# Router on raw rows, expert ranks on 32 partitions, layer 2's expert input by one-hot products

## The chip, the cores and the metric

The kernel runs on one core of one Trainium2 chip. The metric is the device time of one execution in microseconds (us). Three runs of the kernel before are given; where one trace is read, it is one further execution of the same kernel, recorded by the hardware profiler.

## The reference, cut to what matters

Two layers (`DEPTH` 2) over 256 latent tokens (`x`) and 256 context tokens (`ctx`) of width 1024. The context is only needed in the first layer, so layer 0 works on 512 tokens (4 tiles of 128) and layer 1 on 256 (2 tiles). In each layer a mixer gives `y`, and then:

```python
h = layer_norm(alpha * h + g1 * y, ln_g[i, 0], ln_b[i, 0])
f = hier_moe(h * (1 + sc2) + sh2, ...)          # the part that the change is about
h = layer_norm(alpha * h + g2 * f, ln_g[i, 1], ln_b[i, 1])
...
def hier_moe(h, ...):                            # 4 groups of 8 experts, 1024 -> 256 -> 1024
    lg = h @ w_grp + b_grp;  g_sel = argmax(lg)  # one group for each token
    le = h @ w_exp + b_exp                       # 32 expert scores
    top_v, top_i = top_k(le within g_sel, 2)     # two experts for each token
    combine = softmax(top_v) * p_grp
    y += combine[e] * (silu(h @ w_gate[e]) * (h @ w_up[e])) @ w_down[e]
```

With `xhat = (row - mean) * rstd`, the input of the router and of the experts is `xhat * gcol + bcol`, a scale and a shift for each of the 1024 columns that hold `ln_g`, `ln_b`, `sc2` and `sh2`.

## The kernel before

The text counts layers as the code does: `l = 0` and `l = 1` (the change's "layer 2" is `l = 1`). A scheduler places every instruction when the kernel is built; each engine then works through its own list in order, so that an instruction that waits holds back all that stand behind it on its engine.

**Out-projection.** The mixer's output goes through `w_out` in products of 128x512, split into a high and a low part (`ohi`, `olo`), so that three products make one block (lines 191, 192, 193). The halves n = 0 and n = 1 of a tile's 1024 columns are separate sums. After each half, `done(T, n, ps)` (in `post_mixer`) multiplies by the gate `g1` (L1948) and adds to the residual rows `xh` (L1950, L1952) on DVE.

**Normalization and router.** After the half n = 1 of tile T, `ln_stats` gives mean and rstd (`mv`), `ln_scaled` makes the scaled rows `h2` in two operations on 128x1024 (L976, L979), `moe_token_tile` stores `h2` to memory (`h2D`), turns it by 8 transposes (L1026) and multiplies by the router's weights `wr` in 8 fp32 products with 36 columns (L1030; each shows as two records). `ln_hat` writes `xhat` over `xh` on ACT (L984), and `moe_residual` (L1346) multiplies by `alpha * ln_g` and adds `alpha * ln_b` on POOL.

**Routing.** `moe_route` is a chain of small DVE operations: top group, top two experts, one-hot tables `OH`, the counts of each expert (products with the triangle `tri` and with ones), the rank of each expert by count (a compare of all 32 with all 32 on every partition, `big`, L1117 and L1118), the slot of each token's two choices (`slot`, L1139), and tables `idx`, `wt`, `tok`, made by products with one-hot `hl` (L1160, L1161). `perm` is the order of the experts by count.

**Experts.** `plan(l)` packs the experts by rank in passes of one, two or four experts, each pass with 128 slots. Layer 1 has 11 passes. Six experts' weights lie on chip when the routing ends (`SIX`); the others are loaded by SP (three loads of 1 MB each: gate, up, down) as the slots of earlier passes come free. The input of a pass is gathered by row from `h2D` (POOL, indirect DMA) and turned by 8 transposes (L1286). In layer 1 the first three passes (`CHIP1`) instead get theirs by `moe_near`: products of `h2` with a one-hot table `sel` in fp32, 32 records of 128x384 (L1277), after the slots are known. Within a pass, the products of `up` (L1295) run interleaved with the rest of the pass before: turn (L1311), `down` (L1321), sums (L1334); `between` sets that order, and the input of the next pass stands between `down` and the sums.

Of the kernel before, what the change touches and what calls it, by code (L numbers as in the profile page):

```python
# [8 lines left out]
F32 = mybir.dt.float32  # L9
# [9 lines left out]
D = 1024  # L19
# [6 lines left out]
SIX = 6  # L26
# [69 lines left out]
def consts():  # L96
# [55 lines left out]
class Trunk:  # L152
# [784 lines left out]
    def ln_cols(self, l, pool):  # L937
# [4 lines left out]
        o = pool.tile([128, 2, 2, 8], F32, name="lno", tag="lno")  # L942
        eng = nc.gpsimd if l else nc.scalar
        pk = lambda z: z.rearrange("(p k) -> p k", k=8)

        for r in range(2):
            eng.dma_start(c[:, r, 0], pk(self.modD[l][2, r, 0:1024]))
            eng.dma_start(c[:, r, 1], pk(self.modD[l][1, r, 1024:2048]))
        eng.dma_start(g[:, 0], pk(A['ln_g'][l, 0]))
        eng.dma_start(g[:, 1], pk(A['ln_b'][l, 0]))  # L950
        self.gD = gD = self.dp.tile([2, 2, 1024], F32, name=f"gD{l}")
        for r in range(2):
            V.tensor_scalar(c[:, r, 0], c[:, r, 0], 1.0, None, op0=OP.add)
            V.tensor_tensor(o[:, r, 0], g[:, 0], c[:, r, 0], op=OP.mult)
            V.tensor_tensor(o[:, r, 1], g[:, 1], c[:, r, 0], op=OP.mult)
            V.tensor_tensor(o[:, r, 1], o[:, r, 1], c[:, r, 1], op=OP.add)
            for q in range(2):
                eng.dma_start(pk(gD[r, q]), o[:, r, q])
# [28 lines left out]
    def moe_open(self, l, nT):  # L987
# [3 lines left out]
        nc.scalar.dma_start(self.wr[:], A['moe_wr'][l].rearrange("(k p) n -> p k n", p=128))  # L991
        self.br = self.lp.tile([128, 36], F32, name="br")
        self.bcast_row(self.br[:], A['moe_br'][l])
        self.mc = mw.tile([128, 108 + 128 * max(nT, SIX // 2)], F32, name="mc")
# [3 lines left out]
        nc.scalar.dma_start(self.tri[:], A['tri'])  # L998
        self.lg = mw.tile([128, nT, 36], F32, name="lg")
        self.wt = mw.tile([128, 16], F32, name="wt")  # L1000
# [13 lines left out]
        self.h2D = self.dp.tile([128 * nT, D], F32, name=f"h2D{l}")  # L1014
# [3 lines left out]
    def moe_token_tile(self, T, h2, hT):  # L1018

        nc = self.nc  # L1020
        nc.scalar.dma_start(self.h2D[128 * T:128 * T + 128, :], h2)
        for q in range(2):
            pt = self.ps(tag="tr", bufs=2)
            for k in range(4):
                c = 512 * q + 128 * k
                nc.tensor.transpose(pt[:, 128 * k:128 * k + 128], h2[:, c:c + 128], self.ident[:])  # L1026
            self.evac(hT[:, 4 * q:4 * q + 4].rearrange("p a b -> p (a b)"), pt[:], 'a')
        pl = self.ps(tag=("rd", "po")[T % 2], bufs=1)
        for k in range(8):
            nc.tensor.matmul(pl[:, 0:36], hT[:, k], self.wr[:, k], start=k == 0, stop=k == 7)  # L1030
        return lambda: nc.vector.tensor_tensor(self.lg[:, T], pl[:, 0:36], self.br[:], op=OP.add)

    def moe_route(self, l, nT):
# [55 lines left out]
        OH = self.OH  # L1089
        pb = rp.tile([128, 2, nn], F32, name="pb")  # L1090
# [3 lines left out]
        cum = rp.tile([128, nT + 1, 32], F32, name="cum")  # L1094
        both = t(32)
        V.memset(cum[:, 0], 0.0)
        V.tensor_tensor(both[:].rearrange("p t e -> p (t e)"), OH[:, 0], OH[:, 1], op=OP.add)
        for T in range(nT):
            V.tensor_tensor(cum[:, T + 1], cum[:, T], both[:, T], op=OP.add)
        ones = rp.tile([128, 128], F32, name="ones")  # L1100
        V.memset(ones[:], 1.0)
        pn = self.ps()
        nc.tensor.matmul(pn[:, 0:32], ones[:], cum[:, nT], start=True, stop=True)
        pc = self.ps()
        nc.tensor.matmul(pc[:, 0:nn], self.tri[:], both[:].rearrange("p t e -> p (t e)"), start=True, stop=False)
        nc.tensor.matmul(pc[:, 0:nn], ones[:], cum[:, 0:nT].rearrange("p t e -> p (t e)"), start=False, stop=True)

        n1, n2, n4 = WIDE[l]
        cnt, cap = self.cnt, self.cap
        key, rk, b0, t0, t1 = [rp.tile([128, 32], F32, name=n) for n in ("key", "rk", "b0", "t0", "t1")]  # L1110
        big = rp.tile([128, 32, 32], F32, name="big", tag="scr")
        row = lambda z: z.unsqueeze(1).to_broadcast([128, 32, 32])
        col = lambda z: z.unsqueeze(2).to_broadcast([128, 32, 32])
        V.tensor_copy(cnt[:], pn[:, 0:32])
        V.tensor_tensor(key[:], cnt[:], self.mc[:, 32:64], op=OP.mult)
        V.tensor_tensor(key[:], key[:], self.mc[:, 64:96], op=OP.add)
# [3 lines left out]
        V.tensor_scalar(t0[:], rk[:], float(-SIX), 0.0, op0=OP.add, op1=OP.max)  # L1120
        V.tensor_scalar(t0[:], t0[:], float(n1), 64.0, op0=OP.min, op1=OP.mult)
        V.scalar_tensor_tensor(b0[:], rk[:], 64.0, t0[:], op0=OP.mult, op1=OP.add)
        V.tensor_scalar(t0[:], rk[:], float(-SIX - n1 - n2), 0.0, op0=OP.add, op1=OP.max)
# [941 lines left out]
```

## Time and profile before

| | us |
|---|---|
| three runs | 1253.11, 1259.41, 1261.16 (median 1259.41) |
| the profiled execution | 1256.68, its span 1255.0 |
| PE busy | 1022.0 (81%) |
| DVE busy | 600.7 (48%) |
| ACT, POOL busy | 314.4 (25%), 317.3 (25%) |
| DMA queue q1 (weights, SP) | 291.05 MB |
| DMA over the span | 315.66 MB, mean 252 GB/s |

The profiled execution took 1.7 us more than its span. The shares of busy time are averages over stages with different limits: out-projection and expert stage of each layer keep PE or the DMA engines full, and between them lie the heads of the expert stages (normalization, router, routing), in which neither is.

### The profile page before, as it was taken

To read this page: it belongs to the slowest core of one execution; us is meant where nothing else is said; L and a number is where in the kernel's file an instruction comes from. 1 tells how busy PE (TensorE), PEld (TensorE's weight loads), DVE (VectorE), ACT (ScalarE), POOL (GpSimd) and SP (SyncE) were. 2 spreads that over 40 slices of the span, in tenths; PEclk is the share of its full clock that TensorE was granted. 3 is DMA by queue.
4 is the path that set the end of the run, shared out by engine and by line. 5 is a ranking of instruction groups with operands and counts; after the bars stand their busy time and mean duration, and the time that the engine had idled before them with its cause. 6 is when DMAs were issued, how large, how long until landed. Compare 5 with 4: busy or idle time off the path is not lost. (4 is left out here: it accounts for less than half of the span.)

```text
span 1255.0 us, 15029 instructions
## 1 busy us (share of the span) xinstructions
PE 1022.0 (81%) x5440; PEld 568.0 (45%) x5440; DVE 600.7 (48%) x1193; ACT 314.4 (25%) x614; POOL 317.3 (25%) x308
## 2 busy tenths in 40 slices
PE   5679757799899728787777889998999739989775
PEld 2468544355576623232232336655666625433221
DVE  5274894475654861111011172265768574443325
ACT  3143210322443311110000127242346221111001
POOL 7715674263001521110110064014201130000000
PEclk9879978699999959988888889999999859999888
DMA  8442615668295546989999863486344854999992
GB/s 306 168 120 60 216 39 164 181 241 272 70 339 189 221 174 263 410 345 387 408 394 401 326 228 97 159 326 210 120 198 172 318 201 187 411 386 418 419 421 94
DMA packets 78574, 315.66 MB, mean 252 GB/s; under 512 B 15119, under 2 KB 21407, under 8 KB 50272
## 3 DMA queue, kind: packets, MB, share of 16 engines
q1 hardware_dynamic: 61312, 291.05, 60.7%
q0 software_dynamic: 8096, 14.68, 4.2%
q10 hardware_dynamic: 9088, 8.94, 2.3%
q8 instruction: 44, 0.72, 0.2%
q14 instruction: 34, 0.28, 0.1%
HBM read 309.01 MB, written 16.37 MB: 259 GB/s over the span
## 5 line engine op out<-in xcount | busy, mean ns | idle before, releaser
L1295 PE MATMUL ps_mm<-wgu,xT 128*32 128x512 f32 (+2 forms) x960 | 230.8, 651 | 36.9 <-DMA wgu<-in_moe_w_up_dram 36.3
L1295 PEld LDWEIGHTS ps_mm<-wgu,xT 128*32 128x32 f32 (+2 forms) x960 | 58.1, 134 | 151.7 <-issue 140.5
L186 DVE TENSOR_TENSOR wlo<-raw,whi 128x1024 fp32r<-128x1024 f32 (+1 forms) x40 | 50.7, 1275 | 50.7 <-ACT whi L181 50.4
L181 ACT ACTIVATE whi<-raw 128x1024 fp32r<-128x1024 f32 (+1 forms) x42 | 41.5, 999 | 120.4 <-PE ps_rd L192 38.0
L1263 POOL DMA_INDIRECT xg<-h2D,idx x23 | 27.1, 1176 | 151.8 <-PE ps_mod L1334 102.2
L1429 POOL DMA_INDIRECT YD<-ys,dst x13 | 13.1, 1009 | 203.7 <-DVE ys L175 177.7
L193 PE MATMUL ps_mm<-ah,wlo 128*128 128x512 f32 x128 | 51.1, 408 | 14.9 <-DVE wlo L186 14.9
L1321 PE MATMUL ps_mod<-wdn,aT 128*32 128x512 f32 (+2 forms) x240 | 58.1, 674 | 1.0 <-DVE aT L175 1.0
L191 PE MATMUL ps_mm<-ah,whi 128*128 128x512 f32 x128 | 54.7, 430 | 0.8 <-ACT whi L181 0.8
L192 PE MATMUL ps_mm<-al,whi 128*128 128x512 f32 x128 | 52.4, 410 | 0.0
L1321 PE MATMUL ps_rd<-wdn,aT 128*32 128x512 f32 (+2 forms) x240 | 49.2, 593 | 0.0
L192 PE MATMUL ps_mm<-wlo,ah 128*128 128x512 f32 x92 | 39.1, 425 | 9.6 <-DVE wlo L186 8.1
L175 DVE COPY aT<-ps_po 128x256 f32<-128x256 f32 x26 | 11.0, 425 | 71.7 <-PE ps_po L1311 71.7
L1311 PE MATMUL ps_po<-ident,act 128*128 128x128 f32 x52 | 14.3, 363 | 35.6 <-DVE act L1303 35.4
L175 DVE COPY ys<-ps_rd 128x512 f32<-128x512 f32 x13 | 9.0, 692 | 66.7 <-PE ps_rd L1321 66.7
L174 ACT ACTIVATE ys<-ps_mod 128x512 f32<-128x512 f32 x13 | 7.8, 597 | 131.7 <-PE ps_mod L1321 131.7
L1452 DVE COPY dst<-idx 128x1 int32<-128x1 int32 x13 | 1.9, 153 | 80.8 <-DMA YD<-ys,dst 80.8
L193 PE MATMUL ps_mm<-whi,al 128*128 128x512 f32 x92 | 38.6, 419 | 0.6 <-POOL al L669 0.6
L191 PE MATMUL ps_mm<-whi,ah 128*128 128x512 f32 x92 | 38.7, 424 | 0.0
L1346 POOL TENSOR_TENSOR xh<-xh,wdn 128x1024 f32<-128x1024 f32 x12 | 31.3, 2619 | 28.3 <-ACT xh L984 23.6
L181 ACT ACTIVATE ysr<-t 128x512 fp32r<-128x512 f32 x20 | 12.6, 631 | 102.8 <-DVE t L1423 102.8
L175 DVE COPY xT<-ps_tr 128x512 f32<-128x512 f32 (+1 forms) x27 | 18.1, 672 | 38.4 <-PE ps_tr L1286 31.6
(632 smaller groups left out, 2301.8 us busy)
## 6 DMA issues: line engine op xcount, KB each, us to landing
wgu<-in_moe_w_gate_dram SPq DMA_DIRECT2D x60, 1024.0 KB, 7.7
wgu<-in_moe_w_up_dram SPq DMA_DIRECT2D x60, 1024.0 KB, 7.8
wdn<-in_moe_w_down_dram SPq DMA_DIRECT2D x60, 1024.0 KB, 7.6
raw<-in_mod_w_dram SPq DMA_DIRECT2D x24, 1024.0 KB, 5.4
raw<-in_w_in_dram SPq DMA_DIRECT2D x20, 1024.0 KB, 5.2
cc<-in_mod_w_dram SPq DMA_DIRECT2D x16, 1024.0 KB, 5.1
raw<-in_mod_w_dram SPq DMA_DIRECT2D x12, 512.0 KB, 4.8
wgu<-in_w_out_dram SPq DMA_DIRECT2D x4, 1024.0 KB
```

What stands on the lines that cost most here:

```text
L175: return nc.vector.tensor_copy(out, in_)
L181: nc.scalar.activation(hi, x, AF.Copy)
L186: return (nc.gpsimd if leng == 'p' else nc.vector).tensor_tensor(lo, x, hi.bitcast(F32), op=OP.subtract)
L191: mm(ps, l[0], r[0], start=start, stop=False)
L192: mm(ps, l[0], r[1], start=False, stop=False)
L193: mm(ps, l[1], r[0], start=False, stop=stop)
L1263: return self.nc.gpsimd.indirect_dma_start(out=xg, out_offset=None, in_=self.h2D[:], in_offset=bass.IndirectOffsetOnAxis(ap=gi, axis=0), b ...
L1295: self.nc.tensor.matmul(ps[s, :], xT[:, k, s], wts[j][0][:, :, k, :], start=k == 0, stop=k == 7, tile_position=(0, w * j))
L1311: nc.tensor.transpose(pt[:, 128 * k:128 * k + 128], act[:, k::2], self.ident[:])
L1321: self.nc.tensor.matmul(py[s, :], aT[:, k, s], wts[j][1][:, k, 512 * n:512 * n + 512], start=k == 0, stop=k == 1, tile_position=(0, w * j))
L1346: self.nc.gpsimd.tensor_tensor(self.xh[:, T], self.xh[:, T], rows[i], op=op)
L1429: nc.gpsimd.indirect_dma_start(out=self.YD[:], out_offset=bass.IndirectOffsetOnAxis(ap=dst, axis=0), in_=y[:], in_offset=None, bounds_chec ...
```

## The change

- **Router on un-normalized rows.** `router` makes `wrg = wr * gcol` (DVE) and, by products, the constants `lgc` (`gcol` and `bcol` times `wr`): 16 products of 36 columns for each stream, two streams in layer 0, one in layer 1. `router_half` runs after each half of a tile on the raw rows: 4 transposes, a copy, 4 products of 36 columns. The logits are then corrected with mean and rstd by two small operations on DVE. `wr` is laid out so that 576 bytes in a row go to a partition in each piece, where it was 144.
- **`ln_scaled` and the store to `h2D`** remain in layer 0 alone. In layer 1, `hi` and `lo` are the two parts of `xhat` in fp32r (ACT and DVE).
- **Ranks with the experts on partitions.** Counts as a row and as a column (products with ones), a 32x32 compare, and products that spread slot base, end and capacity to all partitions. The operations on 128x1024 are gone.
- **Residual.** Tiles 0 and 1 of layer 0 stay on POOL; tiles 2 and 3 of layer 0 and both tiles of layer 1 are called after the routing and run on DVE, as do three memsets of `xg` in layer 0. Layer 1's memsets are gone.
- **Layer 1's expert input.** All 11 passes by `moe_near`, now 4 products in fp32r for each of 8 column groups, with `gcol` and `bcol` applied in two copies out of PSUM. The first three passes are picked right after the counts (`near`, `sel`), before ranks and slots; the other eight by `moe_pick` from `slot`. The gathers and their transposes are gone there.

```diff
+    def router(self, l, streams):
...
+        for r in streams:
+            w = self.wrg[r] = self.lp.tile([128, 8, 36], F32, name=f"wrg{r}")
+            V.tensor_tensor(w[:], self.wr[:], self.gcol[:, r, 0].unsqueeze(2).to_broadcast([128, 8, 36]), op=OP.mult)
+            c = self.lgc[r] = self.lp.tile([128, 2, 36], F32, name=f"lgc{r}")
+            ps = self.ps(tag="po", bufs=1)
+            for q in range(2):
+                for k in range(8):
+                    nc.tensor.matmul(ps[:, 36 * q:36 * q + 36], self.gcol[:, r, q, k:k + 1].to_broadcast([128, 128]),
+                                     self.wr[:, k], start=k == 0, stop=k == 7)
+            V.tensor_copy(c[:, 0], ps[:, 0:36])
+            V.tensor_tensor(c[:, 1], ps[:, 36:72], self.br[:], op=OP.add)
...
+    def router_half(self, T, r, n, x, hT):
...
+        for j in range(4):
+            nc.tensor.transpose(pt[:, 128 * j:128 * j + 128], x[:, 512 * n + j:512 * n + 512:4], self.ident[:])
+        self.evac(hT[:].rearrange("p a b -> p (a b)"), pt[:], 'a')
+        pl = self.ps(tag=("rd", "po")[n], bufs=1)
+        for j in range(4):
+            nc.tensor.matmul(pl[:, 0:36], hT[:, j], self.wrg[r][:, 4 * n + j], start=j == 0, stop=j == 3)
...
+        pc = self.ps()[:, 0:nn]
+        mm(pc, self.tri[:], both[:].rearrange("p t e -> p (t e)"), start=True, stop=False)
...
+        if l:
...
+            V.scalar_tensor_tensor(near[:], both[:, :, 0:SIX], -1000.0, p3[:, :, 0:SIX], op0=OP.mult, op1=OP.add)
...
+            self.moe_near(sel, self.xT)
...
+        V.tensor_scalar(gt[:], kr[:], kc[:], None, op0=OP.is_lt)
+        pr_ = self.ps()
+        mm(pr_[0:32, 0:32], self.ones[0:32, 0:32], gt[:], start=True, stop=True)
+        mm(pr_[0:32, 32:33], gt[:], self.ones[0:32, 0:1], start=True, stop=True)
...
-        V.tensor_tensor(big[:], row(key[:]), col(key[:]), op=OP.is_gt)
-        V.tensor_reduce(rk[:], big[:], axis=AX.X, op=OP.add)
...
+    def moe_near(self, sel, xT):
...
         for k in range(8):
             pt = self.ps(tag="tr", bufs=2)
             for T in range(2):
-                nc.tensor.matmul(pt[:, 0:n], self.h2[T][:, k::8], sel[:, T], start=T == 0, stop=T == 1)
-            self.evac(self.xT[:, :, k], pt[:, 0:n].rearrange("p (i s) -> p i s", i=CHIP1))
+                for i, z in enumerate((self.hi[T][:], self.lo[T][:])):
+                    self.nc.tensor.matmul(pt[:, 0:n], z[:, k::8], sel[:, T], start=T == 0 and i == 0, stop=T == 1 and i == 1)
...
         if l:
+            self.moe_residual(range(nT), self.lrow, nc.vector)
             self.early((4, 1), (5, 0), (5, 1))
         else:
+            self.moe_residual((2, 3), self.lrow, nc.vector)
+            self.early((1, 1))
...
-            x = (lambda: self.moe_xT(src, xT(i + 1))) if near <= i + 1 < N else None
...
+            elif l and CHIP1 <= i + 1 < N:
+                sel = self.moe_pick(passes[i + 1][1], xp)
+                x = lambda: self.moe_near(sel, xTs(i + 1))
```

What the diff does not tell is where the scheduler puts the moved instructions. DVE in layer 0, around the start of the routing (L979 is the second operation of `ln_scaled`, L1031 the logits), before:

```order
L979 SCALAR_TENSOR_TENSOR wdn<-wdn,mv,B 128x1024
L1031 TENSOR_TENSOR lg<-ps_rd,br 128x36
L983 SCALAR_TENSOR_TENSOR mv<-mv 128x1
L1031 TENSOR_TENSOR lg<-ps_po,br 128x36
L1051 TENSOR_REDUCE rt_3441<-lg 128x4
L1096 MEMSET cum 128x32
```

The same place after (L987 is that second operation, L2017 and L2018 the corrected logits, L1389 the residual, L1083 the first operation of the routing):

```order
L987 SCALAR_TENSOR_TENSOR wdn<-wdn,mv,B 128x1024
L2018 SCALAR_TENSOR_TENSOR lg<-lg,mv,lgc_3001 128x36
L2023 SCALAR_TENSOR_TENSOR mv<-mv 128x1
L1389 TENSOR_TENSOR xh<-xh,wdn 128x1024
L1411 MEMSET xg_3495 128x1024
L1411 MEMSET xg_3496 128x1024
L1411 MEMSET xg_3497 128x1024
L1083 TENSOR_REDUCE rt_3505<-lg 128x4
L1389 TENSOR_TENSOR xh<-xh,wdn 128x1024
L1084 TENSOR_TENSOR rt_3506<-lg,rt_3505 128x16
```

One more L1389 stands before L987 and one more behind L1084: the four residual operations and the three memsets stand in front of the routing's first steps and between them, although the code calls them after it.

DVE in layer 1, the same place, before:

```order
L979 SCALAR_TENSOR_TENSOR xh<-xh,mv,B 128x1024
L1031 TENSOR_TENSOR lg<-ps_rd,br 128x36
L983 SCALAR_TENSOR_TENSOR mv<-mv 128x1
L1031 TENSOR_TENSOR lg<-ps_po,br 128x36
L1051 TENSOR_REDUCE rt_7182<-lg 128x2
```

After:

```order
L2018 SCALAR_TENSOR_TENSOR lg<-lg,mv,lgc_7017 128x36
L2023 SCALAR_TENSOR_TENSOR mv<-mv 128x1
L1389 TENSOR_TENSOR xh<-xh,wdn 128x1024
L2028 TENSOR_TENSOR lo_6996<-xh,hi_6994 128x1024
L1083 TENSOR_REDUCE rt_7289<-lg 128x2
L1389 TENSOR_TENSOR xh<-xh,wdn 128x1024
L1084 TENSOR_TENSOR rt_7290<-lg,rt_7289 128x8
L1093 TENSOR_TENSOR rt_7296<-lg,rt_7289 128x8
L1389 TENSOR_TENSOR xh<-xh,wdn 128x1024
L1085 TENSOR_TENSOR rt_7290<-rt_7290,mc 128x8
L1389 TENSOR_TENSOR xh<-xh,wdn 128x1024
```

The four residual operations of layer 1 and the low part `lo` of tile 1 now stand among the first steps of the routing; the first residual operation needs the row `ln_g` (tile `wdn`) loaded by SP and scaled by ACT.

PE in layer 1's expert stage, one pass, from `down` to the sums, before (`xg` is a gathered tile):

```order
L1321 MATMUL ps_rd<-wdn,aT 64x512 x4
L1295 MATMUL ps_mm<-wgu,xT 64x512 x2
L1286 MATMUL ps_tr<-ident,xg_7164 128x128 x8
L1334 MATMUL ps_mod<-ysr,S 128x512 x2
L1295 MATMUL ps_mm<-wgu,xT 64x512 x2
```

After, the first four of 32 products, which repeat eight times ahead of the sums (L1377):

```order
L1364 MATMUL ps_rd<-wdn,aT 64x512 x4
L1338 MATMUL ps_mm<-wgu,xT 64x512 x2
L1302 MATMUL ps_tr<-sel,hi_6993 128x128
L1302 MATMUL ps_tr<-sel,lo_6995 128x128
L1302 MATMUL ps_tr<-sel,hi_6994 128x128
L1302 MATMUL ps_tr<-sel,lo_6996 128x128
```

In place of 8 transposes PE has 32 products with 128 columns there, in each of eight passes.

## Rows read from the trace of the kernel before

**Rows 1.** Windows: start:end, length; busy PE, PEld, DVE, ACT, POOL; PEclk; DMA share; GB/s.
```profile
368.90:429.40 60.50, 60.43 (x266) 43.84 (x265) 32.86 (x50) 22.02 (x37) 14.38 (x11) 1.00 0.53 200
...
1000.40:1045.00 44.60, 22.67 (x94) 19.97 (x92) 29.50 (x91) 10.70 (x17) 12.11 (x6) 0.66 0.41 159
1045.00:1112.00 67.00, 66.36 (x302) 25.30 (x302) 32.31 (x61) 10.22 (x18) 7.32 (x5) 1.00 0.89 354
1112.00:1234.00 122.00, 102.04 (x505) 32.21 (x503) 41.39 (x73) 12.49 (x22) 4.42 (x3) 0.89 0.94 389
```

**Rows 2.** Timeline of PE in layer 0: start, length, line, tiles, count, idle before.
```profile
373.57 0.39 PE L191 MATMUL ps_mm<-ohi,na 128*128 128x512 f32 x1
...
429.39 1.98 PE L1030 MATMUL ps_rd<-wr,h2T 128*128 128x36 f32 x16
...
439.72 3.63 PE L1030 MATMUL ps_po<-wr,h2T 128*128 128x36 f32 x16
```

**Rows 3.** Router weights: the issue on ACT's queue, and the landing time of both loads.
```profile
371.31 0.39 ACTq L991 DMA_DIRECT2D wr<-in_moe_wr_dram  x1
...
DMA to landing us min/median/max: 6.6/6.6/6.6
```

**Rows 4.** Timeline of DVE in layer 0, from the last product to the slots.
```profile
429.36 0.70 DVE L1948 TENSOR_TENSOR ps_mm<-ps_mm,g 128x512 f32<-128x512 f32 x1 [1.31 <-PE ps_mm L193]
...
445.70 0.17 DVE L1053 TENSOR_TENSOR rt<-rt,mc 128x16 f32<-128x16 f32 x1
...
461.38 0.42 DVE L1139 TENSOR_REDUCE slot<-pb 128x8 f32<-128x256 f32 x1
```

**Rows 5.** Timeline of POOL in layer 0, same stretch.
```profile
445.58 2.73 POOL L1361 MEMSET xg<- 128x1024 f32 x3
```

**Rows 6.** Timeline of PE in layer 1, from the out-projection to the first expert.
```profile
991.87 0.79 PE L192 MATMUL ps_mm<-olo,cc 128*128 128x512 f32 x1 [5.01 <-POOL olo L186]
...
1032.11 12.15 PE L1277 MATMUL ps_tr<-sel,xh 128*128 128x384 f32 x32 [13.96 <-DVE sel L1273]
...
1045.02 2.37 PE L1295 MATMUL ps_mm<-wgu,xT 128*64 128x512 f32 x10
```

**Rows 7.** Timeline of DVE in layer 1, same stretch.
```profile
1000.39 0.70 DVE L1948 TENSOR_TENSOR ps_mm<-ps_mm,g 128x512 f32<-128x512 f32 x1 [2.03 <-PE ps_mm L193]
...
1004.28 1.28 DVE L979 SCALAR_TENSOR_TENSOR xh<-xh,mv,B 128x1024 f32<-128x1024 f32 x1
...
1012.09 0.16 DVE L1054 TENSOR_REDUCE rt<-rt 128x2 f32<-128x8 f32 x1
...
1015.74 0.23 DVE L1097 TENSOR_TENSOR rt<-OH 128x64 f32<-128x64 f32 x1
...
1017.96 3.30 DVE L1117 TENSOR_TENSOR big<-key 128x1024 f32<-128x1024 f32 x1
```

**Rows 8.** Timeline of POOL in layer 1, same stretch.
```profile
989.71 0.23 POOL L1085 TENSOR_SCALAR rec<-mc 128x2 f32<-128x2 f32 x1 [11.64 <-DMA mc<-in_moec_dram]
...
1017.84 10.27 POOL L1346 TENSOR_TENSOR xh<-xh,wdn 128x1024 f32<-128x1024 f32 x4 [4.40 <-ACT wdn L1352]
```

**Rows 9.** Timeline of SP and of ACT in layer 1: row load, its use, weight loads.
```profile
1011.85 0.42 SPq L318 DMA_DIRECT2D wdn<-in_ln_g_dram  x1
...
1110.22 0.34 SPq L161 DMA_DIRECT2D wgu<-in_moe_w_gate_dram  x1
...
1016.70 1.06 ACT L1352 ACTIVATE wdn<-wdn 128x1024 f32<-128x1024 f32 x1 [1.71 <-DMA wdn<-in_ln_g_dram]
```

**Rows 10.** PE in layer 1's expert stage: timeline of two places, and all its waits.
```profile
1074.00 1.16 PE L1286 MATMUL ps_tr<-ident,xg 128*128 128x128 f32 x8
...
1111.96 0.39 PE L1311 MATMUL ps_po<-ident,act 128*128 128x128 f32 x2
...
PE ps_mm L1295 <- DMA wgu<-in_moe_w_up_dram: 20.0, 7, 4.1
```

**Rows 11.** DMA queues from 1112 to 1234: packets, megabytes, share of 16 engines.
```profile
q0 software_dynamic: 432, 0.34, 0.8%
```

More of the change, by code (lines that the diff above doesn't have):

```diff
@@ L1103, in moe_route @@
[L1103 to L1110, printed above, removed]
@@ L1135, in moe_route @@
-        V.scalar_tensor_tensor(at[:], at[:], 100000.0, p3, op0=OP.mult, op1=OP.add)
-        V.tensor_tensor(at[:], at[:], te(b0), op=OP.add)
+        pc = self.ps()[:, 0:nn]
+        mm(pc, self.tri[:], both[:].rearrange("p t e -> p (t e)"), start=True, stop=False)
+        for T in range(nT - 1):
+            mm(pc[:, 32 * T + 32:], self.ones[:], both[:, T:T + 1].to_broadcast([128, nT - 1 - T, 32]), start=False, stop=T == nT - 2)
+        pn = self.ps()
+        for T in range(nT):
+            mm(pn[:, 0:32], self.ones[:], both[:, T], start=T == 0, stop=T == nT - 1)
@@ new lines, in moe_route @@
+        for T in range(nT):
+            mm(pn[0:32, 32:33], both[:, T], self.ones[:, 0:1], start=T == 0, stop=T == nT - 1)
+        p3 = pc.rearrange("p (t e) -> p t e", e=32)
+        if l:
+            near = rp.tile([128, nT, SIX], F32, name="near")
+            sel = rp.tile([128, nT, 64 * SIX], F32R, name="sel")
+            V.scalar_tensor_tensor(near[:], both[:, :, 0:SIX], -1000.0, p3[:, :, 0:SIX], op0=OP.mult, op1=OP.add)
+            for T in range(nT):
+                V.tensor_tensor(sel[:, T].rearrange("p (e s) -> p e s", s=64), self.i64[:].unsqueeze(1).to_broadcast([128, SIX, 64]),
+                                near[:, T].unsqueeze(2).to_broadcast([128, SIX, 64]), op=OP.is_equal)
+            self.moe_near(sel, self.xT)
@@ L1265, in moe_gather @@
                                                  bounds_check=ntok - 1, oob_is_err=False)
-    def moe_near(self, pool):
-        nc, V, n = self.nc, self.nc.vector, 128 * CHIP1
-        sel = pool.tile([128, 2, n], F32, name="sel", tag="scr")
-        for T in range(2):
-            V.tensor_scalar(sel[:, T], self.iota(n), self.slot[:, T:T + 1], None, op0=OP.is_equal)
-            V.scalar_tensor_tensor(sel[:, T], self.iota(n), self.slot[:, 2 + T:3 + T], sel[:, T], op0=OP.is_equal, op1=OP.add)
+    def moe_near(self, sel, xT):
+        n = sel.shape[2]
         for k in range(8):
@@ L1382, in moe_experts @@
         ix = lambda i, c=0: self.idx[:, passes[i][1], c:c + 1]
-        near = CHIP1 if l else 0
-        fetch = lambda i: near <= i < N and self.moe_gather(self.xg[i % 2][:], ix(i), ntok)
-        for i in range(max(near, 2)):
+        fetch = lambda i: l == 0 and i < N and self.moe_gather(self.xg[i % 2][:], ix(i), ntok)
+        for i in range(2):
             g = fetch(i)
```

237 lines of the change are left out of this document (134 added, 103 removed).

## The prediction

> **What bounds the kernel now.** I read the windows first, then the timelines of the engines in the two stretches that the change touches, and last the waits of PE in the expert stage. The windows show that layer 0's out-projection keeps PE full: 60.43 of 60.50 us, 266 records, so about 0.23 us from one to the next, at the full clock of 2.4 GHz (1.00) [rows 1]. Whatever is added to PE there comes out of the end. The heads of the expert stages are the opposite: in layer 1, from 1000.40 to 1045.00, PE is busy half the time, and DMA 41% of it [rows 1]. There DVE's chain of small operations sets the pace, and the reader is to see two things. POOL's residual of 10.27 us starts at 1017.84 [rows 8], and DVE's compare, begun at 1017.96, takes 3.30 us [rows 7], where another operation on 128x1024 takes 1.28 [rows 7]. And the fp32 one-hot products wait for the slots 13.96 us and then take 12.15 us [rows 6].
>
> Layer 1's expert stage has two halves. From 1045 to 1112 PE is busy 66.36 of 67.00 us and DMA moves 354 GB/s; from 1112 to 1234 DMA moves 389 GB/s, and PE waits for weights 20.0 us in 7 places [rows 1, 10]. A weight load is issued when a pass has let go of its slot: the one at 1110.22 [rows 9] comes as pass 4 lets go of its weights, just before the turn at 1111.96 [rows 10] that opens pass 5. So PE sets the pace up to there, and DMA from there on; the end moves with the end of pass 4, not with the first pass alone.
>
> **The change part by part.** The sum is made against the profiled execution, 1256.68 us; its span is 1255.0.
>
> *Layer 0, PE.* Ahead of the last product come the constants, 2 x 16 products of two records (64 records), and 7 of the 8 half tiles, each 4 transposes and 8 records of 36 columns (28 transposes, 56 records). Removed ahead of it are two whole tiles (16 transposes, 32 records) and the third's 8 transposes, whose 16 router records start at 429.39, behind the last product. Sixteen such records take 1.98 us, the end of the last included [rows 2]; I take 0.11 each. 88 more records are 9.7 us. Four more transposes at 0.14 (eight took 1.16 [rows 10]) are 0.6. Nothing covers this: 10.3 us.
>
> The first of the constants needs `wr`. PE reaches it behind the product at 373.57 [rows 2], at about 373.8; `wr` is issued at 371.31 and landed after 6.6 us [rows 3], at 377.9. If the new layout with longer pieces changes nothing, PE stands still 4.1 us; if it lands in half the time, not at all. I take 2, between the two: 12.3 together.
>
> *Layer 0, head.* Before, it was 16.3 us from the gate's multiply (429.36) to the routing's third step (445.70) [rows 4]. After, on DVE: multiply, add and statistics 2.1, one residual operation 1.3 (under PE's half tile), logits of the last half at 5.1 (4 transposes and 8 records at half clock, where 16 records take 3.63 [rows 2], and a copy), small steps 0.3, then `ln_scaled` 2 x 1.28, small steps 0.8, residual 1.3, three memsets, first step and residual 1.5, two steps 0.4, residual 1.3. For the memsets I take POOL's 2.73 us for three [rows 5]. That makes 16.0, a gain of 0.3. The Trainium skill ("VectorE: DVE Perf Modes", section "Zero memsets can be issued as uint32 (trn2)") counts one cycle for an element of a memset; at the 0.96 GHz of that page three would take an estimated 3.2 us, and the gain would be gone. No row shows such a memset on DVE.
>
> The ranks trade five operations on 128x1024 for 18 small fp32 products with DVE steps between them. Twelve products of two records in a row, at half clock (0.23 each [rows 2]), are 5.5 us, and two more short trips to PE and back about 2.5; before, the way from 445.70 to the slots at 461.38 took 15.7 [rows 4]. I take 0.4 gained, bounded by 2 either way. Layer 0 in sum: 12.3 - 0.3 - 0.4 = **11.6 us later**. Its expert stage starts with idle DMA and is passed through unchanged.
>
> *Layer 1, out-projection.* 32 records and three half tiles are 3.5 + 4.3 = 7.8 us more on PE. Against that stand 5.01 us in which PE waited for `olo` [rows 6], which stood behind a POOL instruction that waited 11.64 us for `mc` [rows 8]. The new load of `mc` no longer stands behind 1024 small pieces, and PE comes later, so I take the wait as gone; behind it the products ran some 2 us slower, at half clock, than they would have at full. Net 0, between -1 and +4.
>
> *Layer 1, head.* Before: from the multiply at 1000.39 [rows 7] to the first expert product at 1045.02 [rows 6], 44.6 us. After, counted from the multiply: add at 1.4; logits at 5. The first residual operation on DVE stands ahead of the routing and waits for the row `ln_g`, which SP now issues right after PE's last product. Issue to scaling took 4.85 us (1011.85 to 1016.70) and the scaling 1.06 [rows 9]; with the row before it, 6.8. Then residual and `lo` to 9.3, first step and three residuals with small steps to 13.9; the rest of the routing took 3.9 us, from 1012.09 to 1015.97 [rows 7], to 17.8. This is 2.2 later than before. But now two products, `near` and the first half of `sel` follow, about 2, and the one-hot products begin at 19.7, where they began at 31.7. They are 32 single records of 384 columns in place of two records each for half as many products; at the 0.23 us for 512 columns of the out-projection they would be 0.17 each, 5.5 together, at half clock 11. With the ranks' products among them I take 9.5: first expert product at 29.5 or so. **15 us gained**, between 10 and 19.
>
> *Layer 1, passes.* Passes 2, 3 and 4, ahead of the point where DMA takes over, each get 32 products of 128x128 for 8 transposes of 1.16 us [rows 10]. With 0.12 each, the nearest being records of 128-column weights, they take 3.8 us. Two PSUM buffers serve eight groups; the first copy out stands on ACT behind the split of the second half of `down`, and on DVE behind its low part, which costs another 0.7 or so. I take 3.3 more for each pass, **10 us**, between 1.5 and 6 each (4.5 and 18). The other five passes get the same, but there PE has 20.0 us of waits [rows 10] to put 16.5 in.
>
> The Trainium skill ("TensorE: Matmul & The Clock Gate", section "Back-to-back issue gap") gives 81 ns for a sustained product with 128 columns. By that figure 32 would take an estimated 2.6 us, and the three passes would cost some 6 instead of 10, the sum 4 less. No row here shows such a product.
>
> *Gathers.* From 1112 on they moved 0.34 MB [rows 11], at 389 GB/s 0.9 us; ahead of it DMA has slack. **0.9 gained.**
>
> Sum: 11.6 + 0 - 15 + 10 - 0.9 = +5.7, so 1262 us. The three runs' median, 1259.41, is 2.7 above the profiled one; the range is wide enough for both bases.
>
> **The rivals.** *Cheap products.* If the loads in flight carry DMA through the passes' delay, or the products run near the lower bound, the three passes cost 0 to 4.5: 1252 to 1257. For it: DMA is busy 0.89 even in the first half [rows 1]. Against: PE has no gap there.
> *Dear products (slower).* The eight groups go at the pace of the copies out, which queue on ACT and DVE behind the splits. At 6 us more for each pass the three cost 18: 1270. It is slower by over 1% from 5.7 more in a pass, since that makes 17 of 10.
> *Late rows.* Weight loads are in flight when `ln_g` is issued. If it lands as late as `wr` (6.6) and its second row behind it, DVE waits some 3 to 4 us more ahead of the routing: 1266. This is the case in which the change does not do what it says: the residual, put behind the routing in the code, holds the routing up.
> *Layer 0 for nothing.* If `wr` is there and the short products fit between the long ones, layer 0 costs 2 instead of 11.6: 1252; with cheap products 1243 to 1247. Against it stands the full PE [rows 1].
>
> **How the numbers follow.** Forecast 1258 to 1267: 0.45. Cheap products 0.22, dear products 0.15, late rows 0.08, layer 0 for nothing 0.10. A difference under 1% (12.6 us) is about what a measurement of this kernel can tell from none. Slower by more: most of dear products and a little of late rows, 0.18. Faster by more: layer 0 for nothing with cheap products, or a head that gains 19 and more, 0.12. The rest, 0.70, within. For 8 in 10 the range reaches down to cheap products with some more gained in the head, 1248, and up past dear products, 1274.
>
> **What would show it.** In the trace after: layer 0's gate multiply of the last tile at about 441 to 442 in place of 429.36, with a gap in PE near 374; one-hot products of layer 1 about 20 us behind the last gate multiply; the first expert product 29 to 30 behind it; passes 2, 3 and 4 about 17 us long; DMA not full before pass 5, and full from there on. I am wrong if layer 0's last product comes less than 8 us later, if the head gains less than 10, or if DMA is full from the first pass.

## The result and the profile after

The change makes the kernel slower: 1324.31 us (median of 4 runs, 1318.54 to 1328.17) against 1260.29, ratio 1.051 (95% interval 1.045 to 1.057). The forecast was 1262, no difference. The profiled execution has a span of 1326.5 us, 71.5 more than before.

The span falls into stretches at marks that both traces have. In the table, layer 0's out-projection runs from its first product to the last gate multiply; a head from there to the first expert product; "turns 2 to 5" and "5 to 11" lie between the starts of the turns (L1311 before, L1354 after) in layer 1's expert stage.

| stretch, us | before | after | difference | forecast |
|---|---|---|---|---|
| layer 0 out-projection | 60.0 | 95.0 | +35.0 | +12.3 |
| layer 0 head with ranks | 44.3 | 40.9 | -3.5 | -0.7 |
| layer 1 out-projection | 33.2 | 32.4 | -0.9 | 0 |
| layer 1 head | 44.6 | 36.6 | -8.1 | -15 |
| first expert product to turn 2 | 23.2 | 28.3 | +5.0 | 0 |
| turns 2 to 5 | 43.7 | 69.8 | +26.1 | +10 |
| turns 5 to 11 | 123.4 | 133.3 | +9.9 | -0.9 (gathers) |
| the rest | 882.5 | 890.3 | +7.8 | 0 |

Of the rest, 3.0 lie ahead of the out-projection, whose start varies between 367 and 378 in the kernels of this study, and 4.2 between layer 0's first expert product and layer 1's out-projection, a stretch that takes 489 to 501 us in those with the same routing.

The windows after, by the same columns as [rows 1]:

```profile
372.36:381.44 9.08, 4.63 (x21) 3.52 (x20) 1.24 (x3) 1.24 (x2) 0.27 (x2) 0.87 0.97 384
381.44:423.80 42.36, 42.36 (x124) 29.80 (x125) 5.33 (x12) 7.80 (x13) 0.84 (x4) 0.50 0.05 19
423.80:467.41 43.61, 42.92 (x214) 33.95 (x213) 30.06 (x56) 14.44 (x23) 13.86 (x6) 1.00 0.43 169
1038.28:1074.85 36.57, 18.75 (x70) 16.26 (x71) 23.11 (x84) 11.85 (x21) 0.00 (x0) 0.58 0.41 158
1074.85:1172.93 98.08, 97.47 (x380) 49.61 (x379) 37.77 (x89) 13.85 (x27) 0.00 (x0) 0.86 0.58 227
1172.93:1306.23 133.30, 132.14 (x626) 67.85 (x624) 52.60 (x109) 18.93 (x38) 0.00 (x0) 0.86 0.86 354
```

Two things are new. In layer 0, PE is full from 381.44 to 423.80, but at a granted clock of 0.50, 1.2 GHz. In layer 1, PE is full from the first expert product to the last turn, at 0.86, and DMA is not (0.58 and 0.86 busy); before, PE waited there for weights in the second half [rows 10].

PE in layer 0, timeline, around the constants (L1048), with an out-projection product at either clock:

```profile
376.37 0.39 PE L200 MATMUL ps_mm<-ohi,na 128*128 128x512 f32 x1
376.60 0.39 PE L198 MATMUL ps_mm<-ohi,na 128*128 128x512 f32 x1
381.44 4.88 PE L1048 MATMUL ps_po<-wr,gcol 128*128 128x36 f32 x22 [4.45 <-DMA wr<-in_moe_wr_dram]
...
401.56 0.63 PE L199 MATMUL ps_mm<-olo,wgu 128*128 128x512 f32 x1
401.99 0.63 PE L200 MATMUL ps_mm<-ohi,wgu 128*128 128x512 f32 x1
```

The wait for `wr` is there, 4.45 us; after it, products of 512 columns follow each other at 0.43 us, before it at 0.23.

PE in layer 1, timeline: the start of the first one-hot products, three of the 32 of a pass, and two turns:

```profile
1059.65 0.71 PE L1302 MATMUL ps_tr<-sel,hi 128*128 128x384 f32 x1
...
1103.13 0.51 PE L1354 MATMUL ps_po<-ident,act 128*128 128x128 f32 x2
...
1126.18 0.39 PE L1354 MATMUL ps_po<-ident,act 128*128 128x128 f32 x2
...
1132.20 0.40 PE L1302 MATMUL ps_tr<-sel,hi 128*128 128x128 f32 x1
1132.44 0.40 PE L1302 MATMUL ps_tr<-sel,lo 128*128 128x128 f32 x1
1132.68 0.40 PE L1302 MATMUL ps_tr<-sel,hi 128*128 128x128 f32 x1
```

They start 0.24 us apart; the forecast took 0.12. The spacing is the same at half clock: the last of these 32 still start 0.24 us apart where the window shows 0.50 (busy PE, PEclk, DMA share, GB/s):

```profile
1137.00:1139.40 2.40, 2.40 (x11) 0.50 0.99 403
```

The 32 of a pass take 7.7 to 7.9 us in place of 1.16 for transposes, and the pass between the two turns 23.05 us, where before it took 14.79.

### The profile page after: what moved, and what is told of

Its sections match the earlier page's. It is cut to its first block, busy times and chain, and to the rows that moved or that the text cites. A ratio compares the mean times of both kernels' runs of the same rounds, so it can differ in the third digit from the quotient of the medians.

```text
span 1326.5 us, 15753 instructions
## 1 busy us (share of the span) xinstructions
PE 1119.8 (84%) x5776; PEld 655.1 (49%) x5776; DVE 610.0 (46%) x1266; ACT 330.4 (25%) x648; POOL 284.1 (21%) x290
## 5 line engine op out<-in xcount | busy, mean ns | idle before, releaser
L1338 PE MATMUL ps_mm<-wgu,xT 128*64 128x512 f32 (+2 forms) x624 | 158.4, 657 | 16.4 <-DMA wgu<-in_moe_w_up_dram 15.9
L1338 PEld LDWEIGHTS ps_mm<-wgu,xT 128*64 128x64 f32 (+2 forms) x624 | 42.4, 139 | 93.5 <-issue 82.6
L1338 PE MATMUL ps_mm<-wgu,xh 128*32 128x512 f32 (+2 forms) x336 | 73.8, 675 | 0.0
L1302 PE MATMUL ps_tr<-sel,hi 128*128 128x128 f32 (+1 forms) x144 | 63.0, 438 | 0.0
L1302 PE MATMUL ps_tr<-sel,lo 128*128 128x128 f32 (+1 forms) x144 | 61.6, 428 | 0.0
L1302 PEld LDWEIGHTS ps_tr<-sel,hi 128*128 128x128 f32 x144 | 48.2, 335 | 6.3 <-issue 5.4
L1302 PEld LDWEIGHTS ps_tr<-sel,lo 128*128 128x128 f32 x144 | 48.5, 337 | 0.2
L1354 PE MATMUL ps_po<-ident,act 128*128 128x128 f32 x52 | 13.5, 344 | 34.9 <-DVE act L1346 34.7
L1345 ACT ACTIVATE act<-ps_mm 128x256 f32<-128x256 f32 x26 | 10.0, 383 | 127.6 <-PE ps_mm L1338 127.6
L181 ACT ACTIVATE ys<-ps_mod 128x512 f32<-128x512 f32 x13 | 7.8, 597 | 132.7 <-PE ps_mod L1364 132.7
```

The costliest lines, as they stand in the source:

```text
L1302: self.nc.tensor.matmul(pt[:, 0:n], z[:, k::8], sel[:, T], start=T == 0 and i == 0, stop=T == 1 and i == 1)
L1338: self.nc.tensor.matmul(ps[s, :], xT[:, k, s], wts[j][0][:, :, k, :], start=k == 0, stop=k == 7, tile_position=(0, w * j))
L1345: self.nc.scalar.activation(act[:], ph[:, 0:256], AF.Silu)
L1354: nc.tensor.transpose(pt[:, 128 * k:128 * k + 128], act[:, k::2], self.ident[:])
```

## The experiments

Sixteen kernels. Times with one run are the profiled execution's own; the kernel before lay at 1255 to 1260 beside them. All stretches (us) come from the timelines. e9, e10a and e10b leave work out, and are there to time one stretch; what follows layer 0's out-projection in e9 belongs to another routing, so that its row ends there:

| kernel | L0 out-proj. | L0 head | L1 head | turns 2-5 | 5-11 | time |
|---|---|---|---|---|---|---|
| e1_const_late | 76.2 | 41.7 | 35.1 | 70.2 | 133.4 | 1308.93 |
| e2_before_stall | 83.2 | 44.3 | 46.1 | 43.7 | 122.4 | 1280.11 |
| e9_no_constants | 64.6 | | | | | |
| e15_rows_padded | 81.8 | 42.0 | 36.1 | 69.5 | 132.7 | 1309.39 |
| e16_late_padded | 69.0 | 41.5 | 34.2 | 69.4 | 132.7 | 1292.3 |
| e4_contiguous | 94.2 | 41.7 | 38.9 | 59.0 | 125.0 | 1307.0 |
| e5_256_columns | 95.1 | 41.0 | 36.5 | 64.1 | 126.0 | 1313.62 |
| e6_pairs | 95.3 | 41.0 | 35.6 | 59.5 | 130.2 | 1312.17 |
| e7_combined | 77.7 | 40.8 | 39.8 | 56.0 | 125.0 | 1285.58 |
| e8_old_router_l0 | 60.9 | 43.8 | 36.7 | 54.9 | 127.4 | 1271.09 |
| e10a_no_first_pair | 60.2 | 43.8 | 36.9 | 47.9 | 126.7 | 1258.76 |
| e10b_no_last_pairs | 60.0 | 43.6 | 36.7 | 54.9 | 121.6 | 1263.48 |
| e11_residual_pool | 60.0 | 43.8 | 41.1 | 54.9 | 126.2 | 1278.78 |
| e12_near_then_gather | 60.0 | 43.6 | 43.7 | 44.1 | 123.3 | 1261.69 |
| e14_late_residual | 95.3 | 38.0 | 33.3 | 70.0 | 133.3 | 1318.5 |
| e13_late_near_gather | 60.0 | 41.1 | 35.7 | 44.1 | 122.9 | 1253.1 |

### Layer 0: what holds the clock down

**Constants late.** In `done`, ahead of each stream's first half tile:

```diff
+            if l == 0 and n == 0 and T % 2 == 0:
+                self.router(l, (r,))
```

> The changed kernel, with the router's constants of layer 0 made later: each stream's 16 products are called ahead of its first half tile, so that PE reaches them behind some 24 products of the out-projection instead of behind 3, when wr has landed. Theory (standstill): in the changed kernel PE stood still 4.45 us for wr and then ran at 1.2 GHz until 423.8; it is the standstill after which the clock is low, and without it the out-projection runs at 2.4 GHz. Then the 4.45 us and some 21 us of half speed (42 us at half) are back: about 1324 - 25 = 1299 us, layer 0's first weight load behind the routing near 493 in place of 518.6. Rival (short products): the clock is low because of the 64 records with 36 columns, which stand in the row wherever they are called; then the half clock comes just as long, only later, and the time stays within 6 us of 1324.

**The kernel before with a standstill.**

```diff
+                    nc.tensor.matmul(pw[0:36, 0:36], self.wr[:, 0], self.wr[:, 0], start=True, stop=True)
```

> The kernel before, with one added fp32 product of 36 columns at the place where the changed kernel has its constants; it needs wr, and its result is not used. Theory (standstill): PE stands still some 4 us for wr near 374, then the out-projection runs at 1.2 GHz for 40 us or more, and the time is 20 to 27 us above 1260, about 1284. Rival (short products): one product is no burden, the clock stays at 2.4 GHz, and only the wait itself is lost: 1264.

PE in e2, its one wait for `wr` (timeline) and the windows behind it; then windows of e1 around its 32 constants records:

```profile
379.52 0.30 PE L1999 MATMUL ps_po<-wr 128*36 128x36 f32 x2 [7.25 <-DMA wr<-in_moe_wr_dram]
```

```profile
379.52:415.00 35.48, 35.48 (x69) 20.19 (x70) 5.86 (x9) 9.09 (x15) 1.93 (x5) 0.50 0.00 0
415.00:450.36 35.36, 35.32 (x176) 28.03 (x174) 25.48 (x39) 11.74 (x20) 12.26 (x6) 1.00 0.58 216
```

```profile
389.62:394.40 4.78, 4.78 (x36) 4.09 (x34) 2.42 (x6) 0.96 (x2) 0.00 (x0) 1.00 0.00 0
394.40:404.60 10.20, 10.20 (x35) 7.89 (x35) 1.48 (x5) 3.61 (x6) 0.00 (x0) 0.53 0.01 2
```

A standstill is enough: one product that waits costs the kernel before 23 us, 7.25 of waiting and 35 us at half clock. But it is not needed: in e1 nothing waits, and the clock falls behind the first 32 short records all the same, for 10 us. Both theories held in part; e1 gains 19 us in the stretch, not 25. Nor does every run of short records lower the clock: it stays at 1.00 behind e1's second 32, which start at 413.86, and over layer 1's out-projection in the changed kernel, which has 32 too.

Not every standstill costs as much. In the kernel before, the stage ahead of this one begins with a wait of 2.46 us, and the clock is low behind it for 3.4 us only, among products of 128 rows:

```profile
345.37 0.47 PE L191 MATMUL ps_mm<-zhl,ghi 128*128 128x512 f32 x1 [2.46 <-ACT ghi L181]
```

```profile
345.80:349.20 3.40, 3.40 (x10) 2.66 (x9) 1.86 (x2) 1.70 (x2) 0.00 (x0) 0.50 0.41 123
349.20:360.00 10.80, 10.80 (x49) 8.93 (x49) 6.13 (x8) 7.07 (x11) 0.00 (x0) 1.00 0.97 330
```

**No constants.** `lgc` filled with `br`.

> The changed kernel with the late constants, whose 32 products in layer 0 are left out: lgc is filled with br instead, so that the logits and the routing of layer 0 are others; only its out-projection is to be read. With late constants it took 76.2 us, and the clock was low (0.50) from 395 to 405, just behind the first 32 records with 36 columns, with PE never idle. Theory (short products alone can lower the clock): without the constants the clock stays at 2.4 GHz, 7.3 us of records and some 5 us of half speed go: 63 to 65 us. Rival (the fall has another reason, such as the half tiles' transposes): only the records go, about 69, with the fall still there.

64.6 us, as the theory had it, and the clock never falls:

```profile
372.15:436.76 64.61, 63.92 (x292) 47.31 (x291) 36.44 (x70) 23.35 (x38) 14.99 (x12) 1.00 0.47 182
```

**Row products on 128 rows.** The out-projection of layer 0 has products of 40 rows among its long ones, which spread a row to all partitions; they stand in the kernel before as well. In `rows_open`, with ones in place of zeros below the 40 rows of the data and zeros in the weights there:

```diff
-        pick = pool.tile([32 + n, n], F32R, name="pick")
+        pick = pool.tile([128, n], F32R, name="pick")
```

> The changed kernel, with the products that spread a row to all partitions (the weights are a pick of 40 rows, 512 columns; 11 of them stand between the out-projection's products of layer 0) widened to 128 rows, those beyond the 40th with zero weights. In the changed kernel the clock was at 1.2 GHz from the standstill until 423.5, and the last of these products began at 418.90; in four other kernels it came back 1 to 6 us behind their last one, too. Theory (the narrow products keep the clock down): with 128 rows the clock is full again within some 10 us of the standstill's end, and the out-projection takes 77 to 80 us in place of 95. Rival (they have no part in it): half clock for 42 us as before, 95 us.

> The changed kernel with the constants late and the row products on 128 rows. With the constants late alone, the clock was at 1.2 GHz from 394.4 to 404.6, behind 32 records of 36 columns and among row products of 40 rows, and the out-projection took 76.2 us. Theory (narrow products pull the clock down together): with the row products widened it does not fall, or for less than 5 us, 70 to 73 us. Rival (the 36 columns alone do it): 75 to 77 us.

The standstill of e15, and its windows: standstill, half clock, rest:

```profile
385.75 2.53 PE L1047 MATMUL ps_po<-wr,gcol 128*128 128x36 f32 x11 [5.03 <-DMA wr<-in_moe_wr_dram]
```

```profile
376.25:385.75 9.50, 4.47 (x20) 3.41 (x19) 1.48 (x3) 1.23 (x2) 0.27 (x2) 0.92 1.01 399
385.75:404.40 18.65, 18.65 (x76) 17.59 (x77) 1.38 (x6) 2.39 (x4) 0.84 (x4) 0.50 0.10 37
404.40:458.04 53.64, 52.19 (x262) 41.67 (x260) 34.51 (x61) 19.64 (x32) 13.88 (x6) 1.00 0.37 139
```

The half clock ends after 19 us instead of 42 (10 were expected), though the standstill is as long (5.03 us). In e16 the clock stays at 1.00 behind the first 32 records, which lowered it in e1, and falls behind the second 32, for 3.4 us (busy PE, PEclk, DMA share, GB/s):

```profile
382.85:386.56 3.71, 3.71 (x34) 1.00 0.00 0
404.88:408.30 3.42, 3.42 (x11) 0.53 0.93 369
```

The stretch takes 69.0, less than expected, but not by the clock alone: at full clock a row product and the one behind it took 0.76 us with 40 rows and take 0.49 with 128. So in this stretch a standstill or a run of short records goes ahead of each fall, and the 40-row products that stood among the long ones had a part in how long it lasted. Which run of short records lowers the clock stays open.

### Layer 1: what the one-hot products cost

**Contiguous weights.** `hi` and `lo` stored by column group:

```diff
-    self.nc.tensor.matmul(pt[:, 0:n], z[:, k::8], sel[:, T], ...
+    self.nc.tensor.matmul(pt[:, 0:n], z[:, 128 * k:128 * k + 128], sel[:, T], ...
```

> The changed kernel, with hi and lo of layer 1 stored by column group, so that the weights of each one-hot product are 128 elements in a row instead of every eighth. In the changed kernel 32 such products with 128 columns follow each other at 0.24 us, and a weight load shows 0.34 us, where the out-projection's show 0.19. Theory (stride): the load of strided weights sets the 0.24; with contiguous ones the pitch falls to 0.15 or less, 8 passes x 32 x 0.09 = 23 us and more: 1301 or below. Theory (width): a product of fp32r with 128 columns costs as much as an fp32 one in two records, whatever the layout; the pitch stays at 0.24 and the time within 5 us of 1324.

**256 columns.** `sel` and its compare twice as wide.

> The changed kernel, with every one-hot product of passes 4 to 11 of layer 1 given 256 columns instead of 128; the second half is computed and not read. Theory (width): the wider product leaves the dear regime: 384 columns took 0.32 us at 1.2 GHz, so one column a cycle, and 256 columns at 2.4 GHz would take 0.11 to 0.15; the time falls by 8 x 32 x 0.1 = 25 us to about 1299 although the columns are doubled. Theory (stride): the weight load sets 0.24, and twice the columns cost nothing or something more: 1324 to 1350.

Weight loads by line (count, busy, mean ns) after, then in e4; then two products of e4:

```profile
L1302 PEld LDWEIGHTS ps_tr<-sel,lo 128*128 128x128 f32 x144 | 48.5, 337 | 0.2
```

```profile
L1302 PEld LDWEIGHTS ps_tr<-sel,lo 128*128 128x128 f32 x144 | 29.8, 207 | 0.5 <-issue 0.5
```

```profile
1107.41 0.28 PE L1302 MATMUL ps_tr<-sel,lo 128*128 128x128 f32 x1
1107.52 0.28 PE L1302 MATMUL ps_tr<-sel,hi 128*128 128x128 f32 x1
```

Stride it is: with contiguous weights the products start 0.11 us apart; with 256 columns and stride, 32 still take 7.8 to 8.0. e4's time of 1307 misses the 1301 expected, since its 32 products take 4.9 to 6.0 us and not 3.6: between the groups PE waits for copies out of PSUM, up to 0.5 us at a time. And e5 is 16 us shorter in the stage, which neither theory had. The windows show why; 32 products and what follows them, after, then in e5 (busy PE, PEclk, DMA share, GB/s), and last all of e5 from turn 2 to 5:

```profile
1131.50:1139.40 7.90, 7.90 (x34) 0.84 1.01 415
1139.40:1148.80 9.40, 9.40 (x34) 0.77 0.29 92
```

```profile
1128.60:1136.60 8.00, 8.00 (x35) 1.00 1.01 420
1136.60:1143.80 7.20, 7.20 (x33) 1.00 0.31 108
```

```profile
1101.60:1165.70 64.10, 64.10 (x276) 38.29 (x275) 29.27 (x63) 10.42 (x21) 0.00 (x0) 1.00 0.64 248
```

With 128 columns at 0.24 us each, the clock falls at the end of the 32 and stays low behind them, as behind short records in layer 0; with 256 it stays full.

**Two passes at a time.**

```diff
+                sel = self.moe_pick([passes[i + q][1] for q in (1, 2)], xp)
+                x = lambda: self.moe_near(sel, xTs(i + 1) + xTs(i + 2))
```

> The changed kernel, with the expert input of passes 4 to 11 of layer 1 made for two passes at a time: 32 products with 256 columns, all used, in front of every second pass, in place of 32 with 128 columns in front of each; the weights stay strided. Theory (the strided weight load sets 0.24 us, whatever the columns, as with 256 of them before): 4 x 32 x 0.24 = 31 us in place of 61, so that from the first expert product to the last turn it takes about 231 - 30 = 201 us, in all some 1294. Rival (copies out): the eight groups go at the pace of the copies out of PSUM, which are twice as many to a group; then little is gained, 1310 to 1324. No less than the 190 us of the kernel before can come of it, since its PE waited 20 us for weights.

**All three edits, and the old router in layer 0.**

> Three edits at once: the constants of layer 0 late, contiguous weights, and two passes at a time. If each gain stands by itself: layer 0's out-projection 76 us in place of 95 (-19), the expert stage of layer 1 with 4 x 32 x 0.113 = 15 us of products in place of 61, less what DMA then holds back, 193 to 197 us in place of 231 (-36): 1324 - 55 = 1269 us, still some 1% above the kernel before by the short products of layer 0. Rival (copies out set the pace of the groups): 205 us and more, 1280.

> As the combined kernel, but layer 0's router as in the kernel before: whole tiles of scaled rows, 8 transposes and 8 products, no constants; the ranks on partitions, the residual behind the routing and layer 1's new head stay. By the stretches measured so far: layer 0's out-projection 60 us in place of 95 (-35), its head within 3 of before, layer 1's out-projection and head 41 + 32 in place of 78 (-9 against the kernel before), its expert stage 193 to 197 against 190: in all about 1251 to 1256 against 1256 to 1260 of the kernel before, a gain of 0.5% or less. Rival: the time that layer 1's head gains is given back in the expert stage, where DMA sets the pace: no difference.

PE's waits in e8 from 1050 to 1300:

```profile
PE ps_mm L1359 <- DMA wgu<-in_moe_w_up_dram: 17.4, 5, 4.0
PE ps_tr L1320 <- DVE xh L1326: 3.9, 9, 1.0
```

A pair's 32 products take 8.7 to 9.3 us in e6, and turns 5 to 11 gain little by it, since PE waits there for weights again (16.4 us). In e8 a pair takes 7.0, of which 32 products 0.12 apart are 3.8; the rest lies between its eight groups, where the next needs a PSUM buffer that has been copied out. That was the rival in e6 and e7, and both came out at its times (1312 and 1286). e8 came out above both of its own, at 1.2% more than the kernel before: its expert stage took 209 us where 193 to 197 were expected.

**A pair, or two, left out of e8.**

> The kernel with layer 0's old router, contiguous weights and pairs, with the one-hot products of the first pair (the input of passes 4 and 5 of layer 1) left out; those passes work on what lies in their buffers. Theory (the first half decides): up to the fifth turn PE sets the pace, so the 6 us that pass 2's 32 products cost come back in full, from the first expert product to the last turn 209 - 6 = 203 us, and some 1265 in all. Rival (DMA sets the pace throughout): the weights come no earlier, 207 to 209 us, 1271.

> The same kernel with the last two pairs left out instead (the input of passes 8 to 11): 64 products, twice as many as in the run without the first pair. Theory (the first half decides): behind the fifth turn PE waits 17.4 us for weights, and the products only fill that time; 206 to 209 us from the first expert product to the last turn, 1268 to 1271 in all. Rival (every product costs, wherever it stands): 12 us less, 197 us and 1259.

What is left out is the 32 products with their table and their copies. Ahead of turn 5 that shortens turns 2 to 5 by 7.0, all that the products took; two pairs behind it give 5.8 of 14 us. So the place decides, as forecast, but the later ones are hidden by no more than some 60%, and e10b comes out between its theory and its rival.

**Residual on POOL.** `nc.vector` to `nc.gpsimd` in e8.

> The kernel with layer 0's old router, contiguous weights and pairs, with layer 1's residual on POOL instead of DVE, still called behind the routing. In the changed kernel DVE stood 2.25 us for the scaled row ahead of the routing and then spent 4 x 1.2 us on the residual among its first steps. Theory (late rows): with DVE free of it the routing and the first expert product come 6 to 7 us earlier, 1264 to 1266. Rival (POOL slows DVE down, as in the kernel before, where an operation of 1.3 us took 3.3 beside it): 0 to 2 us, 1269 to 1272.

Two first steps of the routing on DVE, 128x8, beside POOL:

```profile
1024.53 2.13 DVE L1102 TENSOR_TENSOR rt<-lg,rt 128x8 f32<-128x8 f32 x1
...
1026.69 2.27 DVE L1103 TENSOR_TENSOR rt<-rt,mc 128x8 f32<-128x8 f32 x1
```

They take 0.15 to 0.16 otherwise (in e8), a third such step takes 2.19, and the head is 4.4 us longer. The rival's mechanism is right and its size too small: POOL costs more there than the residual on DVE.

**Near products, then gathers; residual really late.**

> As the kernel with the residual on POOL, but passes 4 to 11 of layer 1 get their input by gathers again (rows of xhat stored to memory, gathered, 8 transposes, scaled on the way out of PSUM); only the first three passes keep the one-hot products out of the counts. Theory: the expert stage is as in the kernel before, 190 to 193 us from first product to last turn in place of 209, and the head stays short: 1271 - 17 - 6 = 1248 us or up to 1252, below both kernels. Rival (the gathers come late, since the rows are stored only behind the normalization and the buffers are hi's): 200 us and more, 1258 and above.

> The changed kernel with one edit: the residual operations on DVE (two tiles in each layer) are held until the routing's table idx is made, so that they stand behind the routing in DVE's list and not among its first steps. Theory (late rows and residual): in layer 1 the wait of 2.25 us for the scaled row and four operations of 1.2 us leave the way to the first expert product, 36.6 - 7 = 29.5 us; in layer 0 four operations of 1.3 us leave the head, 40.9 - 5 = 36. Together 10 to 12 us, 1312 to 1314. Rival (the chain is not set by DVE there, or the residual only moves ahead of the first pass's products): the heads within 2 us, 1322 to 1326.

> The kernel with layer 0's old router, the near products and gathers for the other passes, with layer 1's residual on DVE instead of POOL and the residual of both layers held until idx is made. Theory: layer 1's head 43.7 - 14 = 29 to 31 us, layer 0's 43.6 - 5 = 38.5, the expert stage 192 to 195 (one weight load waits for the rows' tile): 1262 - 17 = 1243 to 1247 us, faster than both kernels by 1%. Rival (the weight load that waits for the tile of the rows, or the gathers, come later by as much as the head is shorter): 1254 to 1260, no difference from the kernel before.

```diff
+            with tc.issue_after(self.routed):
                 self.moe_residual(range(nT), self.lrow, nc.vector)
```

Held back until `idx`, the residual makes layer 0's head 2.9 us shorter and layer 1's 3.2, half of what was expected; `lo` still waits ahead of the routing, for ACT, which makes `hi`, scales a row and then makes `xhat` (DVE's timeline of e14):

```profile
1038.80 1.23 DVE L2030 TENSOR_TENSOR lo<-xh,hi 128x1024 fp32r<-128x1024 f32 x1 [3.39 <-ACT xh L2028]
```

With gathers the stage is as before (44.1 and 123 us). e12 nevertheless misses its 1248 to 1252, since its head, with the residual on POOL, takes 43.7 us. e13 comes out half a percent below the kernel before: 1253.1 us, ratio 0.995 (0.992 to 0.998), 12 runs. That is less than its forecast of 1243 to 1247, as layer 1's head takes 35.7 us and not 29 to 31, and as little as the kernel before moved from one set of runs to the next. It keeps the ranks, the late residual, layer 1's router on raw rows and the near products.

## Why the prediction was wrong

*Layer 0, PE: mis-sized, by a cost that the sum did not have.* The added records were nearly right: at full clock the 64 of the constants take 7.1 us (e1), and the half tiles add 4.6 (e9, 64.6 against 60.0), 11.7 where 10.3 were forecast. `wr` landed in about 7 us as before, not in half the time, so the wait was 4.45 where 2 were taken. The 18.9 that are left of the 35.0 are what the working lacked, the clock: 42.36 us at half speed can lose up to 21.2. The step that failed is "I take 2, between the two", which priced a standstill by its length alone; [rows 1] show 1.00 for the stretch, and no chance was given to its fall. The trace before gave no hint of 42 us, though: 20.0 us of waits in seven places [rows 10] go there with a clock of 0.89 over 122 us [rows 1], an estimated 27 us at half clock for all seven together. "I am wrong if layer 0's last product comes less than 8 us later" looked to the wrong side; the sign "if the head gains less than 10" did show, with 8.1.

*Layer 1, passes: mis-sized.* "With 0.12 each, the nearest being records of 128-column weights" fits weights that lie in a row (0.11 in e4); products with those of `z[:, k::8]` start 0.24 us apart, shown by e4 and e5. Passes 2, 3 and 4 got 8.3 to 9.1 us longer, beyond the upper bound of 6. 6.6 is the products (7.8 less 1.16); the rest goes with the clock, since in e5, with products as long and the clock at 1.00, the three got 6.8 longer each. *Dear products* had the right sign and the wrong mechanism: the copies out set the pace only after the weights were mended. The structure stood: what is added ahead of turn 5 counts in full (e10a). "The other five passes get the same, but there PE has 20.0 us of waits [rows 10] to put 16.5 in" failed by size and by the clock again: five times 6.6 is 33, and 9.9 stuck out, but only 2.6 in e5. DMA did not fill behind pass 5 (0.86), since PE, busy for 132.14 of 133.30 us, set the pace there too.

For the 81 ns of the Trainium skill ("TensorE: Matmul & The Clock Gate", section "Back-to-back issue gap"), which the prediction set beside its 0.12: contiguous weights give 0.11, strided ones 0.24; the measurements decide.

*Layer 1, head: right mechanism, half the size.* The one-hot products began 21.4 us behind the gate multiply (forecast 19.7): the first residual operation came at 9.2 and not at 6.8, as the row landed 6.2 us behind its issue and was scaled behind `hi` on ACT. That is *Late rows*, with 2.25 us of waiting in place of 3 to 4. From there to the first expert product it took 15.2, forecast 9.5: at half clock 32 records 0.32 apart are 10.2, near the 11 given for it, and the ranks' products stand between them. Besides, turn 1 comes 14.5 us behind the first expert product and not 9.4: six of the eight records of the `idx` table now stand behind that product, where all stood ahead of it, and the clock over this stretch is 0.76. In e1, with the same order at 1.00, it is 11.2, so the clock has the larger part. Counted to turn 1 the head gained 3.0.

*Right:* layer 1's out-projection (-0.9, forecast 0), by the mechanism named: the wait for `olo` is gone and the clock is 1.00, where it was 0.90. Nearly right: layer 0's head, 3.5 gained where 0.7 were forecast, half of it in the ranks and inside their bound of 2. The three memsets on DVE, for which no row stood, are 0.91 each with 0.16 between them, 2.98 from the first to the step behind them: between the 2.73 of the sum and the 3.2 set beside it.

Not settled: what in a product the clock answers to. e15 and e16 changed the rows of one kind, e5 the columns of another, and the same 32 short records lowered the clock in one place and not in another. The clock's part in layer 1's stage is read from e5 and was not tried by itself.

## What to carry to other kernels

Before a product is put into a full row of TensorE, look at what its weights look like in memory, and price it from a record with that layout. A standstill or a burst of small products can cost what follows it too: before taking it at its own length, ask how long the clock stayed low behind such a place elsewhere in the trace, and whether the same kind of products stood behind it there. In the trace before it was 3.4 us among products of 128 rows; among those of 40 rows it became 42. Let a new operand's load be called early enough, or its first user late; that alone was worth 19 us in its stretch here, and 15 in the whole time (e1).

## What was not expected of the hardware

- A standstill of PE of 4.45 us was followed by 42 us at 1.2 GHz with PE busy all the time; 18.65 us, behind 5.03 of standstill, once the 40-row products used 128 rows; 3.4 us behind a standstill of 2.46 with no 40-row products about.
- One-hot products in fp32r with every eighth element as weights: 0.24 us apart with 128 and with 256 columns; 0.11 to 0.12 with contiguous weights, at either width. The 0.24 is the same at 1.2 and at 2.4 GHz.
- Beside POOL's residual, three DVE steps of 128x8 took 2.1 to 2.3 us in place of 0.15.
